# Low parts of the ordinary feed-forward blocks by ScalarE and an adding transfer, and ten more pairs of blocks in seven products

## The chip, the core and the metric

One core of a Trainium2 chip runs the whole kernel. The metric is the device time of one execution in microseconds; three runs of the kernel before gave 1870.56 us at the median (1868.07 to 1871.55). TensorE multiplies, VectorE and ScalarE do elementwise work, GpSimd does a little of it and can issue transfers, SyncE (SP) issues the loads.

## The reference

Two decoder layers over 512 tokens of 1024 channels in float32, batch 1. Each layer is a SwiGLU half-step, a mixer, and another SwiGLU half-step; so there are four feed-forward blocks in all. Every sub-layer is an RMSNorm, a shift and scale from the conditioning vector `c` (adaLN, nine vectors of 1024 a layer, each a 1024 x 1024 product with `c`), and a gated residual add:

```
h = modulate(rms_norm(x, ffn_norm[i, 0]), mod[:, 0, 0], mod[:, 0, 1])
x = x + 0.5 * mod[:, 0, 2][:, None, :] * swiglu(h, w_gate, w_up, w_down)
# swiglu: (silu(h @ w_gate) * (h @ w_up)) @ w_down, d_ff = 2816
```

The mixer of layer 0 is a convolution module beside a gated short convolution, that of layer 1 a causal pooling beside block-sparse attention. A last RMSNorm follows.

## The kernel before

**Numbers.** Activations lie transposed: 8 tiles `x[k]` of 128 channels x 512 tokens. TensorE multiplies in a reduced float32 kind (fp32r), so every operand is split in a high part (a cast) and a low part (the value minus the high part), and a product of two is three matmuls: high x high, high x low, low x high (`mac`, L295).

**Ordinary blocks.** An `Item` is one weight block, K x 128 columns, K = 1024 for gate and up. Two items share one `Raw`, a load of 128 partitions x 2048 floats from HBM into one of four buffers (`RAW_BUFS`), issued on SP's queue in the order in which the plan first touches it; a load goes out only when the buffer of the fourth load before it has been used up. `split` (L270) makes the parts: ScalarE casts the high part (L284), VectorE subtracts for the low part (L286; GpSimd for a few marked ones). The parts have four buffers (`W_BUFS`), and `run` splits up to three items ahead (`AHEAD`) of the one that is multiplied, as soon as the item four back has been emitted. Then come 24 matmuls of 512 columns and `post`: SiLU for gate, the product with it for up (`m`, then its split in `th`, `tl`), the residual for down.

**Pairs.** A gate block and the up block beside it, taken as a 2 x 2 block matrix by the halves of K and by the tokens' halves, can be done in seven products instead of eight (`pair_run`, L817): 84 matmuls of 256 columns instead of 48 of 512. For that VectorE forms sums of weights (`sums13`, `sum2`, `sum4`), splits them, and recombines the results; of the activations `forms` (L717) makes sums once per feed-forward block. The d_ff of 22 blocks of 128 is cut in sections of 8, 6 and 8; in each a number of gate/up blocks, the last ones, go in pairs. The counts before are (0, 2, 8), (2, 6, 8), (2, 4, 8), (2, 6, 8) for the four feed-forward blocks, 56 pairs.

**Order.** Engines run their queues in order, and the order is written out by a plan. `swiglu_pairs` (L948) goes through a feed-forward block: the ordinary gate/up items of a section, then its pair run, then the down items. Beside ordinary items (`beside`) it puts steps of other work for VectorE: the four `forms`, the four `lead_in` steps of the next pair run, and background steps, above all the adaLN products (`ada_steps`, L466: per vector four loads of 1 MB with two VectorE passes each, a fold, a reduce). How many go beside an item is set by a credit in us (3.7 for a gate or up item, 3.5, 2.3 or 2.9 for a down item), from which each step's cost is taken. Around a change of sub-layer `boundary` (L585) weaves the last two down items with the first four items of the next.

Of the kernel before, what the change touches and what calls it, by code (L numbers as in the profile page):

```python
# [42 lines left out]
class Item:  # L43


    def __init__(self, raw, cut, shape, post=None, rhs=None, korder=None, store=None):
        self.raw, self.cut, self.shape = raw, cut, shape
        self.post, self.rhs = post, rhs
        self.korder, self.store = korder, store
        self.hi = self.lo = self.ps = None  # L50
        self.left = 0
        self.pool_low = self.late = self.hold = False
# [16 lines left out]
class Trunk:  # L69
# [183 lines left out]
    def load(self, r):  # L253
        n = 1
        for s in r.shape[1:]:
            n *= s
        t = self.raw.tile([P, 2048], F32, name="raw", tag="raw")[:, 0:n]
        if isinstance(r.src, tuple):
            r.tile = t.rearrange("p (g k c) -> p g k c", g=2, k=ND)
            for g in range(2):  # L260
                self.nc.sync.dma_start(r.tile[:, g], r.src[g])
        elif len(r.shape) == 4:
            r.tile = t.rearrange("p (a b c) -> p a b c", a=r.shape[1], b=r.shape[2])
            for b in range(r.shape[2]):
                self.nc.sync.dma_start(r.tile[:, :, b, :], r.src[:, :, b, :])
        else:
            r.tile = t.rearrange("p (a b) -> p a b", a=r.shape[1])
            self.nc.sync.dma_start(r.tile, r.src)

    def split(self, it):  # L270
# [10 lines left out]
        for i, (hi, lo) in enumerate(parts):  # L281
            w = src[:, i * step:(i + 1) * step, :]
            n = w.shape[1]
            self.nc.scalar.copy(hi[:, 0:n, :], w)  # L284
            eng = self.nc.gpsimd if it.pool_low else self.nc.vector
            low = lambda eng=eng, lo=lo, hi=hi, w=w, n=n: eng.tensor_tensor(  # L286
                lo[:, 0:n, :], w, hi[:, 0:n, :].bitcast(F32), op=ALU.subtract)
            if it.hold:
                self.held.append(low)
            else:  # L290
                low()
            it.hi += [hi[:, a, :] for a in range(n)]
            it.lo += [lo[:, a, :] for a in range(n)]
# [235 lines left out]
    def square(self, k, sl):  # L529

        nc = self.nc
        if k == 0:
            nc.scalar.activation(self.acc[:, sl], self.x[k][:, sl], AF.Square)
            return
        sq = self.np_.tile([P, S], F32, name="sq", tag="sq")
        nc.scalar.activation(sq[:, sl], self.x[k][:, sl], AF.Square)
        if self.ending and k == 7 and sl.start > 0:
            self.sq7 = sq
            return
        self.defer(lambda: nc.vector.tensor_tensor(  # L540
            self.acc[:, sl], self.acc[:, sl], sq[:, sl], op=ALU.add))

    def stats(self, half):
        nc = self.nc
        ps = self.bank()
        for j in range(2):
            c = 2 * half + j
            terms = [self.acc] if half == 0 or not self.ending else [self.acc, self.sq7]
            for t in terms:
                nc.tensor.matmul(ps[:, j:j + 1], lhsT=t[:, c * P:(c + 1) * P], rhs=self.ones[:, 0:1],  # L550
                                 start=t is terms[0], stop=t is terms[-1])
# [95 lines left out]
    def pair(self, src, nk, posts, apart=False, **kw):  # L647

        if apart:
            return [Item(Raw([P, nk, P], src[:, :, j * P:(j + 1) * P], 1), (lambda t: t), (nk, P),  # L650
                         post=posts[j], **kw) for j in range(2)]
        r = Raw([P, nk, 256], src, 2)
        return [Item(r, (lambda t, j=j: t[:, :, j * P:(j + 1) * P]), (nk, P), post=posts[j], **kw)
                for j in range(2)]

    def ffn_items(self, l, s):
# [8 lines left out]
        for n, nf in enumerate(SECTIONS):  # L665
            gu = []
            for fp in range(nf // 2):
# [7 lines left out]
                def up_post(slot):  # L675
                    def go(ps, sl):
# [12 lines left out]
                              apart=apart)  # L689
                u = self.pair(wu[:, :, c0:c0 + 256], ND, [up_post(q) for q in sl_], rhs=self.h_rhs,  # L690
                              apart=apart)
                gu += [g[0], u[0], g[1], u[1]]
            down = []
            for dp in range(ND // 2):
# [3 lines left out]
                    rhs=self.t_rhs)  # L698
# [118 lines left out]
    def pair_run(self, pairs, down):  # L817
# [17 lines left out]
        def keep1(p):  # L835
            p.p1 = self.fp.tile([P, 256], F32, name="p1c", tag="p1c", bufs=1)
# [110 lines left out]

    def swiglu_pairs(self, secs, pairs, bg, skip, fn=None, due=0):  # L948
# [5 lines left out]
        lead = [list(zip(self.lead_in(ps[0]), (2.5, 1.4, 1.9, 1.2))) if ps else [] for ps in pairs]  # L954
        for n, ((gu, down), ps) in enumerate(zip(secs, pairs)):
# [190 lines left out]
    def group_norm(self, r):  # L1146
        nc = self.nc
        _, j, y, stage, x = r
        if stage == 0:
# [4 lines left out]
            r[4] = sq = self.np_.tile([P, S], F32, name="sq", tag="sq")  # L1154
            nc.scalar.activation(sq, y, AF.Square)
        elif stage == 1:
# [9 lines left out]
            r[4] = wide = self.np_.tile([P, S], F32, name="sq", tag="sq")  # L1166
# [115 lines left out]
    def pool_post(self, g):  # L1282
        nc = self.nc

        def go(ps, sl):
# [9 lines left out]
            def mean():  # L1295
                o = self.np_.tile([P, S], F32, name="sq", tag="sq")
# [6 lines left out]
            def mix(o):  # L1303
# [3 lines left out]
                m = self.np_.tile([P, S], F32, name="sq", tag="sq")  # L1307
# [163 lines left out]
    def start_spread(self):  # L1471
# [5 lines left out]
        self.rb0 = self.np_.tile([P, S], F32, name="sq", tag="sq")  # L1477
# [46 lines left out]
    def build(self):  # L1524
# [66 lines left out]
        self.swiglu_pairs(f[0, 0], self.pair_items(0, 0, (0, 2, 8)), bg, 7, AF.Sigmoid, 9)  # L1591
# [46 lines left out]
        bg = steps(1, (2, 0), (2, 2))  # L1638
# [18 lines left out]
        self.swiglu_pairs(f[1, 2], self.pair_items(1, 2, (2, 6, 8)), [], 3)  # L1657
# [102 lines left out]
```

## Time and profile before

| | us |
|---|---|
| median of 3 runs | 1870.56 |
| the profiled execution | 1867.62 |
| its span, first to last instruction | 1865.6 |
| TensorE busy | 1803.4 |
| VectorE busy | 1438.5 |
| ScalarE busy | 802.3 |
| GpSimd busy | 133.9 |

The profile is of one execution. Matmuls are pipelined, so "busy" says that TensorE had work, not that it ran at its peak; what a matmul costs on the path is the distance from its start to the next one's. An engine that waits shows it as idle time, with the instruction that ended the wait behind it. A DMA share of 1 means that all 16 DMA engines moved packets the whole time.

### The profile page before, as it was taken

To read this page: it belongs to the slowest core of one execution; us is meant where nothing else is said; L and a number is where in the kernel's file an instruction comes from. 1 tells how busy PE (TensorE), PEld (TensorE's weight loads), DVE (VectorE), ACT (ScalarE), POOL (GpSimd) and SP (SyncE) were. 2 spreads that over 40 slices of the span, in tenths; PEclk is the share of its full clock that TensorE was granted. 3 is DMA by queue.
4 is the path that set the end of the run, shared out by engine and by line. 5 is a ranking of instruction groups with operands and counts; after the bars stand their busy time and mean duration, and the time that the engine had idled before them with its cause. 6 is when DMAs were issued, how large, how long until landed. Compare 5 with 4: busy or idle time off the path is not lost.

```text
span 1865.6 us, 26636 instructions
## 1 busy us (share of the span) xinstructions
PE 1803.4 (97%) x10730; PEld 1566.0 (84%) x10730; DVE 1438.5 (77%) x2100; ACT 802.3 (43%) x1388; POOL 133.9 (7%) x107
## 2 busy tenths in 40 slices
PE   5999999999979999999999999999999999999998
PEld 4778889988758888989888889998876688898997
DVE  6689779788988868779678787886898577485874
ACT  4322335445544433535344234463545444253543
POOL 2100000005550000000000000000002000000000
PEclk7999999999989999999999999999999999999999
DMA  9585563433232346453423573543362132424321
GB/s 258 169 290 198 161 204 101 136 113 113 68 136 91 113 158 181 133 139 113 149 77 114 191 226 119 156 124 111 125 208 80 45 91 68 113 80 125 91 91 46
DMA packets 263234, 247.52 MB, mean 133 GB/s; under 512 B 5212, under 2 KB 243656, under 8 KB 263112
## 3 DMA queue, kind: packets, MB, share of 16 engines
q1 hardware_dynamic: 262980, 245.78, 42.5%
q8 instruction: 84, 1.38, 0.3%
q14 instruction: 38, 0.31, 0.0%
q10 hardware_dynamic: 132, 0.05, 0.0%
HBM read 243.72 MB, written 2.10 MB: 132 GB/s over the span
## 4 chain that ended last, share of the span: by engine, by line
PE 82%; DVE 12%; ACT 3%; issue 2%; POOL 1%; DMA 0%; SPq 0%; DVEq 0%; ACTq 0%; POOLq 0%
PE bank L784 27%; PE bank L299 17%; PE bank L301 17%; PE bank L300 17%; DVE hl L577 1%; DVE wlo L286 1%; DVE bank L1111 1%; PE bank L1378 1%; DVE wlo L753 1%; DVE t L572 1%; DVE adaacc L484 1%; ACT whi L284 1%; DVE s L762 1%; DVE acc L1501 1%; DVE yb L1043 0%
## 5 line engine op out<-in xcount | busy, mean ns | idle before, releaser
L299 PE MATMUL bank<-th,whi 128*128 128x512 f32 (+1 forms) x896 | 336.3, 375 | 5.2 <-ACT whi L284 4.5
L301 PE MATMUL bank<-th,wlo 128*128 128x512 f32 (+1 forms) x896 | 332.8, 371 | 5.4 <-POOL wlo L286 5.4
L300 PE MATMUL bank<-tl,whi 128*128 128x512 f32 (+1 forms) x896 | 332.8, 371 | 1.1 <-DVE tl L680 0.9
L299 PE MATMUL bank<-hh,whi 128*128 128x512 f32 (+1 forms) x864 | 322.3, 373 | 5.3 <-ACT hh L575 3.2
L300 PE MATMUL bank<-hl,whi 128*128 128x512 f32 (+1 forms) x864 | 316.8, 367 | 8.0 <-DVE hl L577 8.0
L301 PE MATMUL bank<-hh,wlo 128*128 128x512 f32 (+1 forms) x864 | 315.9, 366 | 2.5 <-DVE wlo L286 2.5
L284 ACT CAST whi<-raw 128x1024 fp32r<-128x1024 f32 (+1 forms) x205 | 203.9, 1010 | 136.3 <-PE bank L300 83.2
L286 DVE TENSOR_TENSOR wlo<-raw,whi 128x1024 fp32r<-128x1024 f32 (+1 forms) x195 | 235.0, 1220 | 26.5 <-ACT whi L284 25.7
L301 PEld LDWEIGHTS bank<-th,wlo 128*128 128x128 f32 x896 | 169.0, 189 | 38.5 <-POOL wlo L286 6.6
L299 PEld LDWEIGHTS bank<-th,whi 128*128 128x128 f32 x896 | 169.1, 189 | 38.0 <-ACT whi L284 5.6
L300 PEld LDWEIGHTS bank<-tl,whi 128*128 128x128 f32 x896 | 169.2, 189 | 32.2 <-DVE tl L680 1.3
L300 PEld LDWEIGHTS bank<-hl,whi 128*128 128x128 f32 x864 | 164.0, 190 | 37.9 <-DVE hl L577 9.5
L299 PEld LDWEIGHTS bank<-hh,whi 128*128 128x128 f32 x864 | 163.5, 189 | 37.5 <-ACT hh L575 3.3
L988 DVE SCALAR_TENSOR_TENSOR x<-bank,modG,x 128x512 f32<-128x512 f32 (+1 forms) x124 | 85.7, 698 | 141.1 <-PE bank L301 140.1
L301 PEld LDWEIGHTS bank<-hh,wlo 128*128 128x128 f32 x864 | 163.6, 189 | 32.2 <-DVE wlo L286 3.7
L784 PE MATMUL bank<-f,whi 128*128 128x256 f32 x896 | 163.7, 280 | 11.2 <-ACT yy L843 11.2
L784 PE MATMUL bank<-f,qhi 128*128 128x256 f32 x896 | 165.3, 282 | 0.0
L741 ACT CAST qhi<-raw 128x512 fp32r<-128x512 f32 x168 | 99.4, 618 | 118.4 <-issue 84.4
L784 PEld LDWEIGHTS bank<-f,whi 128*128 128x128 f32 x896 | 136.8, 188 | 13.4 <-ACT yy L843 13.4
L484 DVE SCALAR_TENSOR_TENSOR adaacc<-raw,cond,adaacc 128x1024 f32<-128x1024 f32 x112 | 143.7, 1283 | 2.7
L784 PEld LDWEIGHTS bank<-f,qhi 128*128 128x128 f32 x896 | 138.8, 190 | 0.0
L784 PE MATMUL bank<-f,qlo 128*128 128x256 f32 x448 | 126.4, 282 | 0.0
(245 smaller groups left out, 3317.8 us busy)
## 6 DMA issues: line engine op xcount, KB each, us to landing
raw<-in_ada_w_dram SPq DMA_DIRECT2D x64, 1024.0 KB, 5.3
raw<-in_ffn_w_down_dram SPq DMA_DIRECT2D x32, 1024.0 KB, 5.2
raw<-in_ffn_w_gate_dram SPq DMA_DIRECT2D x58, 512.0 KB, 4.0
raw<-in_ffn_w_up_dram SPq DMA_DIRECT2D x58, 512.0 KB, 5.3
raw<-in_ffn_w_gate_dram SPq DMA_DIRECT2D x15, 1024.0 KB, 5.4
raw<-in_ffn_w_up_dram SPq DMA_DIRECT2D x15, 1024.0 KB, 5.4
raw<-in_ffn_w_down_dram SPq DMA_DIRECT2D x16, 768.0 KB, 4.5
raw<-in_conv_w_in_dram SPq DMA_DIRECT2D x10, 1024.0 KB, 5.0
```

The source lines that it names most:

```text
L284: self.nc.scalar.copy(hi[:, 0:n, :], w)
L286: low = lambda eng=eng, lo=lo, hi=hi, w=w, n=n: eng.tensor_tensor(lo[:, 0:n, :], w, hi[:, 0:n, :].bitcast(F32), op=ALU.subtract)
L299: nc.tensor.matmul(ps, lhsT=it.hi[k], rhs=xh[:, sl], start=start, stop=False)
L300: nc.tensor.matmul(ps, lhsT=it.hi[k], rhs=xl[:, sl], start=False, stop=False)
L301: nc.tensor.matmul(ps, lhsT=it.lo[k], rhs=xh[:, sl], start=False, stop=stop)
L484: nc.vector.scalar_tensor_tensor(acc, r.tile[:, j, :], self.cond[:, k:k + 1], acc, op0=ALU.mult, op1=ALU.add)
L572: nc.vector.scalar_tensor_tensor(t, self.x[k][:, sl], self.modA[:, i, k:k + 1], rb, op0=ALU.mult, op1=ALU.mult)
L577: self.pend = lambda: nc.vector.scalar_tensor_tensor(self.hl[k][:, sl], t, b, self.hh[k][:, sl].bitcast(F32), op0=ALU.add, op1=ALU.subtract)
L741: self.nc.scalar.copy(hi, src)
L753: p.lows[names] = lambda: self.nc.vector.tensor_tensor(lo, src, hi.bitcast(F32), op=ALU.subtract)
L784: mm = lambda w, x, start=False: nc.tensor.matmul(ps, lhsT=w, rhs=x, start=start, stop=False, skip_group_check=True)
L988: nc.vector.scalar_tensor_tensor(self.x[d][:, sl], ps[:, sl], self.modG[:, i, d:d + 1], self.x[d][:, sl], op0=ALU.mult, op1=ALU.add)
```

## The change

`split` gets a third way for marked items (`by_dma`): ScalarE writes the negated cast into the low part's tile, and a transfer issued by GpSimd adds the weights to it, SBUF to SBUF. `swiglu_pairs` marks the gate/up items that are not taken in a boundary and all down items. So that the transfer's source is one row of 4 KB in each partition, ordinary loads are made as two, each of 128 columns (`whole`). The counts of pairs become (0, 4, 8) and three times (4, 6, 8). Where a section has fewer items than steps, `join` puts several steps behind one item. The credits become 4.7 and 4.6, 3.2 or 4.0. One adaLN vector (layer 1, sub-layer 2, scale) moves from the third feed-forward block to the attention. Some scratch tiles change their pool or tag, and the scratch for GpSimd's transfers is 2048 bytes instead of 1024.

```diff
@@ split @@
-            if it.hold:
+            if it.by_dma:
+                self.nc.scalar.activation(lo[:, 0:n, :], w, AF.Copy, scale=-1.0)
+                self.nc.gpsimd.dma_start(lo[:, 0:n, :], w, accum_op=ALU.add)
+            elif it.hold:
                 self.held.append(low)
@@ load @@
-            r.tile = t.rearrange("p (g k c) -> p g k c", g=2, k=ND)
+            r.tile = t.rearrange("p (g k c) -> p g k c", g=2, c=P)
@@ pair @@
-        r = Raw([P, nk, 256], src, 2)
-        return [Item(r, (lambda t, j=j: t[:, :, j * P:(j + 1) * P]), (nk, P), post=posts[j], **kw)
-                for j in range(2)]
+        if whole:
+            r = Raw([P, 2, nk, P], (src[:, :, 0:P], src[:, :, P:2 * P]), 2)
+            cuts = [lambda t, j=j: t[:, j] for j in range(2)]
+        else:
+            r = Raw([P, nk, 256], src, 2)
+            cuts = [lambda t, j=j: t[:, :, j * P:(j + 1) * P] for j in range(2)]
+        return [Item(r, cuts[j], (nk, P), post=posts[j], **kw) for j in range(2)]
@@ ffn_items @@
-                              apart=apart)
+                              apart=apart, whole=(n, fp) > (0, 0))
...
-                    rhs=self.t_rhs)
+                    rhs=self.t_rhs, whole=True)
@@ new @@
+    def join(self, forms, lead, n):
+        gap = n - len(forms) - len(lead)
+        if gap >= 0:
+            return forms + [(None, 0)] * gap + lead
+        out = [(None, 0)] * (n - 4) + lead
+        for e, (fn, cost) in enumerate(forms):
+            k = e * (n - 3) // len(forms)
+            f0, c0 = out[k]
+            if k < n - 4:
+                out[k] = (lambda a=f0, b=fn: (a and a(), b()), c0 + cost)
+            else:
+                last = forms[e:]
+                out[k] = (lambda b=f0: ([f() for f, _ in last], b()), c0 + cost * len(last))
+                break
+        return out
@@ swiglu_pairs @@
+        for it in secs[0][0][max(skip + 1, 4):] + sum((gu * (n > 0) + down for n, (gu, down) in enumerate(secs)), []):
+            it.by_dma = True
...
-                todo = forms + [(None, 0)] * (len(gu) - 8) + todo
-            self.beside(gu, todo, bg, 3.7)
+                todo = self.join(forms, todo, len(gu))
+            self.beside(gu, todo, bg, 4.7)
...
-                        2.9 if last else 3.5 if nf == 8 else 2.3)
+                        4.0 if last else 4.6 if nf == 8 else 3.2)
@@ square, keep1, group_norm, pool_post, start_spread: tiles @@
-        sq = self.np_.tile([P, S], F32, name="sq", tag="sq")
-        nc.scalar.activation(sq[:, sl], self.x[k][:, sl], AF.Square)
+        if sl == FULL:
+            sq = self.fp.tile([P, S], F32, name="yy", tag="yy", bufs=2)
+        else:
+            sq = self.np_.tile([P, 256], F32, name="sq", tag="sq")
+        nc.scalar.activation(sq, self.x[k][:, sl], AF.Square)
...
-            p.p1 = self.fp.tile([P, 256], F32, name="p1c", tag="p1c", bufs=1)
+            p.p1 = self.np_.tile([P, 256], F32, name="t256", tag="t", bufs=3)
@@ build @@
-        self.swiglu_pairs(f[0, 0], self.pair_items(0, 0, (0, 2, 8)), bg, 7, AF.Sigmoid, 9)
+        self.swiglu_pairs(f[0, 0], self.pair_items(0, 0, (0, 4, 8)), bg, 7, AF.Sigmoid, 9)
...
-        self.swiglu_pairs(g0, self.pair_items(0, 2, (2, 6, 8)), bg, 3)
+        self.swiglu_pairs(g0, self.pair_items(0, 2, (4, 6, 8)), bg, 3)
...
-        bg = steps(1, (1, 1), (1, 0), (1, 2), (2, 1))
-        self.swiglu_pairs(f[1, 0], self.pair_items(1, 0, (2, 4, 8)), bg, 3, AF.Exp)
+        bg = steps(1, (1, 1), (1, 0), (1, 2))
+        self.swiglu_pairs(f[1, 0], self.pair_items(1, 0, (4, 6, 8)), bg, 3, AF.Exp)
...
-        bg = steps(1, (2, 0), (2, 2))
+        bg = steps(1, (2, 1), (2, 0), (2, 2))
...
-        self.swiglu_pairs(f[1, 2], self.pair_items(1, 2, (2, 6, 8)), [], 3)
+        self.swiglu_pairs(f[1, 2], self.pair_items(1, 2, (4, 6, 8)), [], 3)
...
-                    dynamic_dma_scratch_size=1024)
+                    dynamic_dma_scratch_size=2048)
```

## Rows read from the trace of the kernel before

**Rows 1.** Page: busy us, share of span, instructions; then the chain by engine
```profile
PE 1803.4 (97%) x10730; PEld 1566.0 (84%) x10730; DVE 1438.5 (77%) x2100; ACT 802.3 (43%) x1388; POOL 133.9 (7%) x107
...
PE 82%; DVE 12%; ACT 3%; issue 2%; POOL 1%; DMA 0%; SPq 0%; DVEq 0%; ACTq 0%; POOLq 0%
```
**Rows 2.** Waits of TensorE: engine, line, awaited; us in total, times, longest
```profile
PE bank L784 <- ACT yy L843: 11.2, 11, 2.8
PE bank L300 <- DVE hl L577: 8.0, 6, 1.6
```
**Rows 3.** Windows: stretch, length, busy us by engine, PEclk, DMA share, GB/s
```profile
620.00:630.00 10.00, 10.00 (x44) 8.07 (x43) 9.65 (x18) 3.74 (x7) 0.00 (x0) 1.00 0.31 107
295.00:305.00 10.00, 10.00 (x88) 10.00 (x87) 9.09 (x13) 5.97 (x13) 0.00 (x0) 1.00 0.40 107
```
**Rows 4.** Windows of the first feed-forward block
```profile
95.00:105.00 10.00, 10.00 (x44) 8.04 (x43) 8.83 (x9) 2.83 (x4) 0.00 (x0) 1.00 1.05 376
140.00:150.00 10.00, 9.80 (x43) 7.99 (x44) 9.45 (x15) 2.11 (x2) 0.00 (x0) 1.00 1.00 349
83.40:147.00 63.60, 62.65 (x271) 50.21 (x272) 56.40 (x71) 18.99 (x25) 0.00 (x0) 1.00 0.81 282
```
**Rows 5.** Timeline of ScalarE in a pair run: start us, us, instruction
```profile
300.48 0.37 ACT L837 COPY p1c<-bank 128x256 f32<-128x256 f32 x1
...
310.30 0.37 ACT L837 COPY p1c<-bank 128x256 f32<-128x256 f32 x1
```
**Rows 6.** Timeline of TensorE in ordinary items
```profile
621.43 0.40 PE L299 MATMUL bank<-hh,whi 128*128 128x512 f32 x1
...
626.33 0.39 PE L299 MATMUL bank<-hh,whi 128*128 128x512 f32 x1
```
**Rows 7.** Page, costliest groups: xcount, busy us, mean ns, idle before
```profile
L284 ACT CAST whi<-raw 128x1024 fp32r<-128x1024 f32 (+1 forms) x205 | 203.9, 1010 | 136.3 <-PE bank L300 83.2
L286 DVE TENSOR_TENSOR wlo<-raw,whi 128x1024 fp32r<-128x1024 f32 (+1 forms) x195 | 235.0, 1220 | 26.5 <-ACT whi L284 25.7
...
L484 DVE SCALAR_TENSOR_TENSOR adaacc<-raw,cond,adaacc 128x1024 f32<-128x1024 f32 x112 | 143.7, 1283 | 2.7
```
**Rows 8.** Page, DMA issues: xcount, KB each, median us to landing
```profile
raw<-in_ffn_w_gate_dram SPq DMA_DIRECT2D x58, 512.0 KB, 4.0
```
**Rows 9.** Timeline of ScalarE at the start of the second feed-forward block
```profile
610.25 2.00 ACT L284 CAST whi<-raw 128x1024 fp32r<-128x1024 f32 x2
```
**Rows 10.** Timeline of TensorE there
```profile
615.13 0.39 PE L299 MATMUL bank<-hh,whi 128*128 128x512 f32 x1
615.36 0.40 PE L300 MATMUL bank<-hl,whi 128*128 128x512 f32 x1
615.60 0.39 PE L301 MATMUL bank<-hh,wlo 128*128 128x512 f32 x1
```
**Rows 11.** Timeline of SP's queue, first feed-forward block
```profile
69.18 14.63 SPq L268 DMA_DIRECT2D raw<-in_ada_w_dram  x2
...
141.31 0.37 SPq L268 DMA_DIRECT2D raw<-in_ffn_w_down_dram  x1
```
**Rows 12.** Timeline of TensorE, first matmul of the seventh down block
```profile
169.22 0.39 PE L299 MATMUL bank<-th,whi 128*128 128x512 f32 x1
```
**Rows 13.** Windows in the attention
```profile
1400.00:1420.00 20.00, 20.00 (x82) 13.56 (x81) 17.66 (x37) 10.25 (x24) 10.35 (x9) 1.00 0.19 65
1420.00:1440.00 20.00, 20.00 (x83) 13.79 (x82) 14.48 (x31) 11.62 (x26) 1.43 (x1) 1.00 0.18 54
```

More of the change, by code (lines that the diff above doesn't have):

```diff
@@ L51, in __init__ @@
         self.left = 0
-        self.pool_low = self.late = self.hold = False
+        self.pool_low = self.late = self.hold = self.by_dma = False
 class Pair:
@@ L540, in square @@
         self.defer(lambda: nc.vector.tensor_tensor(
-            self.acc[:, sl], self.acc[:, sl], sq[:, sl], op=ALU.add))
+            self.acc[:, sl], self.acc[:, sl], sq, op=ALU.add))
     def stats(self, half):
@@ L549, in stats @@
             for t in terms:
-                nc.tensor.matmul(ps[:, j:j + 1], lhsT=t[:, c * P:(c + 1) * P], rhs=self.ones[:, 0:1],
+                e = j if t is not self.acc else c
+                nc.tensor.matmul(ps[:, j:j + 1], lhsT=t[:, e * P:(e + 1) * P], rhs=self.ones[:, 0:1],
                                  start=t is terms[0], stop=t is terms[-1])
@@ L645, in t_rhs, with pair @@
         return self.th[k], self.tl[k]
-    def pair(self, src, nk, posts, apart=False, **kw):
+    def pair(self, src, nk, posts, apart=False, whole=False, **kw):
         if apart:
@@ L688, in ffn_items @@
                 g = self.pair(wg[:, :, c0:c0 + 256], ND, [gate_post(q) for q in sl_], rhs=self.h_rhs,
-                              apart=apart)
+                              apart=apart, whole=(n, fp) > (0, 0))
                 u = self.pair(wu[:, :, c0:c0 + 256], ND, [up_post(q) for q in sl_], rhs=self.h_rhs,
-                              apart=apart)
+                              apart=apart, whole=(n, fp) > (0, 0))
                 gu += [g[0], u[0], g[1], u[1]]
@@ L1153, in group_norm @@
             self.free(ps)
-            r[4] = sq = self.np_.tile([P, S], F32, name="sq", tag="sq")
+            r[4] = sq = self.fp.tile([P, S], F32, name="sqw", tag="sqw", bufs=2)
             nc.scalar.activation(sq, y, AF.Square)
@@ L1165, in group_norm @@
             nc.gpsimd.tensor_tensor(rs, ms, self.mhalf, op=ALU.pow)
-            r[4] = wide = self.np_.tile([P, S], F32, name="sq", tag="sq")
+            r[4] = wide = self.fp.tile([P, S], F32, name="sqw", tag="sqw", bufs=2)
             nc.scalar.copy(wide.rearrange("p (a b) -> p a b", a=8), rs[:, :, None].to_broadcast([P, 8, 64]))
@@ L1295, in mean @@
             def mean():
-                o = self.np_.tile([P, S], F32, name="sq", tag="sq")
+                o = self.fp.tile([P, S], F32, name="sqw", tag="sqw", bufs=2)
                 nc.vector.scalar_tensor_tensor(o, cur[:, 16:], 1.0 / w, u[:, 16:],
@@ L1306, in mix @@
                 b, sc = self.at["pool_b"] + g, self.at["pool_scale"] + g
-                m = self.np_.tile([P, S], F32, name="sq", tag="sq")
+                m = self.fp.tile([P, S], F32, name="sqw", tag="sqw", bufs=2)
                 nc.vector.tensor_scalar(m, po, self.vec[:, b:b + 1], self.vec[:, sc:sc + 1],
@@ L1476, in start_spread @@
                                 self.rs[0][:, c:c + 1].to_broadcast([P, P]), self.ident)
-        self.rb0 = self.np_.tile([P, S], F32, name="sq", tag="sq")
+        self.rb0 = self.fp.tile([P, S], F32, name="yy", tag="yy", bufs=2)
         nc.scalar.copy(self.rb0, ps)
```

## The prediction

> **What bounds the kernel now.** I read the page's busy times and its chain of waits first. TensorE is busy 97% of the span and holds 82% of the chain [rows 1]; the reader is to see that nothing else is near. The list of what TensorE waited for then shows how little idle time there is: the longest entry is 11.2 us in 11 waits of the `f` products, the next 8.0 us [rows 2]. So a gain has to come from fewer TensorE columns. VectorE is the engine that limits how many blocks can go in seven products: in a run of pairs it is busy 9.09 of 10 us, and in the ordinary stretch of the first section 9.65 of 10 [rows 3]. The share of the DMA engines is the third view: small on average, but in the first feed-forward block it is 1.05 at 376 GB/s in one stretch of 10 us and 1.00 at 349 GB/s in another [rows 4]. The change takes load off VectorE and puts it on the DMA engines, so the question is what that costs there.
>
> **The seven products: the gain.** In the run of eight pairs the copy of p1 comes once a pair: from 300.48 to 310.30 us is 9.82 us a pair [rows 5]. An ordinary gate or up block is 24 matmuls of 512 columns. From 621.43 to 626.33 us are 21 of them, 0.233 us each, so two blocks take 48 x 0.233 = 11.20 us [rows 6]. The saving is 1.38 us a pair. The counts go from 10+16+14+16 = 56 to 12+18+18+18 = 66 pairs: 10 x 1.38 = 13.8 us less on TensorE, all of it on the path. The number of pair runs stays 11, so the stall of the first pair of each run (the 11 waits above) stays too.
>
> **The low parts: off VectorE, on ScalarE.** With `by_dma` an item's low part is a second ScalarE pass (1.01 us by the high part's row) in place of 1.22 us of VectorE [rows 7], and a transfer issued by GpSimd. Marked and run are 8+4+24 items in the first block (gate/up of two sections, and all down blocks) and 4+24 in each of the other three, 120 in all: 146 us leave VectorE, 121 us come to ScalarE, which is busy 43% [rows 1]. I cost ScalarE's part at nothing where splits run three items ahead (16.8 us), and VectorE's relief also at nothing: TensorE did not wait for it there, and the credit per item (3.7 to 4.7 us and so on) fills the relief with the adaLN steps that lost their places. Adding up those credits by the code, every step still finds a place before its end. GpSimd waits for ScalarE at each issue; behind that stand only the two small powers of the statistics and the third head block's low part, which come after the last marked items of a block.
>
> **The adding transfer itself.** Its kind does not stand in the trace. The nearest rows are loads: 512 KB lands 4.0 us after issue at the median [rows 8]; at the full-share rates of [rows 4] (349 to 376 GB/s) 512 KB holds the 16 engines for 1.45 us. An add needs source and destination, so up to two such passes: 2.9 us. Ends therefore 1.45 and 2.9 us of the engines, landing after 4.0 to 5.4 us. At nothing I do not put the low end: the bytes have to move; what could make it nothing on the path is idle DMA time.
>
> **Where the transfer is waited for.** At a block's start the first marked item's buffer becomes free only when TensorE is done with the first head item. In the trace of before, ScalarE's cast of it begins at 610.25 (two casts in a row of 2.00 us), and TensorE wants its low part at 615.60 [rows 9, 10]. In the changed order cast and negated copy end at 612.3, which leaves 3.3 us for a landing of 4.0 to 5.4: 0.7 to 2.1 us late, in three blocks 2 to 6.3 us. I take 6. It covers another squeeze: five items now have to carry eight steps that had nine items (four `forms` at 4.6 us and four lead-in steps, 25.4 us by the code's own costs, behind the first item's end), 22.4 us of TensorE; what VectorE is late there, 2 to 3 us, falls into the same wait. Later items have 11 us or more, the first down block of a run nearly 10: no wait at landings up to 7 us.
>
> **The first feed-forward block.** Here the sum of DMA time decides. From 83.4 us to 147.0 the DMA share was 0.81, so 51.5 us of the engines, for 11 adaLN loads and 6 weight loads of 1 MB, the last of which, for the last two down blocks, was issued at 141.31 [rows 4, 11]: 3.0 us a load. The changed code asks for more before that same weight load: by the credits 16 adaLN loads precede it, one of them already issued at 69.18, so 4 more, 12 us. Weight rows shrink from 1 KB to 512 bytes (two loads of 512 KB): 10 us at a share of 0.40 and 107 GB/s where rows have 512 bytes, against 0.31 for the same bytes in 1 KB rows [rows 3], 0.9 us a MB, 5 us for six. And 13 adding transfers, 19 to 38 us. Together 87.5 to 106.5 us. The seventh down block's products begin at 169.22 [rows 12]; back from there 2 us of ScalarE and 5.4 of landing, so its load must be in by about 162: 78.6 us. The engines are over-asked by 9 to 28 us, and because loads share four buffers in program order, weights cannot pass the adaLN loads. I take 14, nearer the low end: a load's 3.0 us holds waits for HBM, which a transfer inside SBUF may fill. Elsewhere the demand fits: the other blocks have 5.6 us an item and at most one adaLN load for each.
>
> The Trainium skill, "Collectives: The Full Stack", section "The bandwidth ceiling: the fold count and why AG ≠ RS ≠ AR", says that an add in the DMA engines is slower than a copy because it takes two source reads, pushed through one read queue. No run here shows it yet. By it the estimate is the upper end, 28 us in this stretch, and the sum below would be 23 us over; by the copy rows alone it would be the lower one, 9 us.
>
> **The moved adaLN set.** One more set (eight VectorE passes of up to 1.28 us [rows 7], by the code's costs a fold of 2.8 and a reduce of 0.9: 13.9 us) runs beside the attention, reaching to about 1420 us. VectorE is there busy 17.66 of 20 us, then 14.48 [rows 13]. It falls behind by up to 11 us and needs to be in time only two units (some 8 us) later. 0 to 11 us late; I take 3. Tags and scratch size move no work: nothing. The second issue of each weight load is 0.37 us more on SP's queue [rows 11], which stands idle between loads: nothing.
>
> **Sum.** -13.8 + 6 + 14 + 3 = +9.2 us on the profiled execution's 1867.6 us. That execution stands 2.9 us under the median 1870.56, so against the median 1880.
>
> **Rivals.**
> (a) The transfers hide, and the change is faster. Place: the same stretch of the first block. Of its first 63.6 us 19% of DMA time is free [rows 4], and the share goes over 1.00, so transfers inside SBUF may run while loads wait for HBM; if an adding transfer costs the loads under about 0.7 us, the over-demand falls to 2 us or less, and with landings of 4.0 us: -13.8 + 2 + 2 + 1 = -8.8, 1862. For it: the relief of VectorE is real and TensorE's saving certain. Against: the full stretches of [rows 4].
> (b) One pass per transfer, nothing hidden: -13.8 + 2 + 9 + 1 = -1.8, 1869: no change.
> (c) Two full passes: -13.8 + 6.3 + 28 + 3 = +23.5, 1894. Should a transfer land after more than 7 us, each pair run's end waits as well.
> (d) The change does not carry its pairs: adaLN steps left over at a block's end would be done with TensorE idle, 2.6 us each. The credits speak against it; I give it no share of its own.
>
> **How the numbers follow.** Forecast 0.36, (a) 0.33, (b) 0.14, (c) 0.17. Under 0.2% (3.7 us, about what a measurement of this kernel tells from no change) lies (b) with its edges: 0.14. Faster 0.33, slower 0.53. The forecast's own range is 1875 to 1888. For eight in ten I reach from 1860, near (a)'s value with its best edge (every unknown at its low end and no over-demand: -11.8) left out, to 1898, past (c) but short of all upper ends together (-13.8 + 6.3 + 28 + 11 = +31.5).
>
> **What would show it.** Right: most of the loss before 180 us; from 95 to 165 us the DMA share near 1.0 throughout, TensorE waiting for low parts that a DMA brought or for weights, VectorE waiting for adaLN loads; pair periods unchanged at 9.8 us; at each later block's start one wait of 1 to 2 us of the L301 products. Wrong: adding packets of under half the time of a 4 KB load, no idle TensorE before 180 us, and the saving of 13.8 us bare; or waits at every down block, which would make it worse than (c).

## The result and the profile after

The changed kernel takes 1936.96 us (median of 4 runs, 1936.07 to 1938.48) where the kernel before took 1871.05 beside it (4 runs, 1868.07 to 1871.96): a ratio of 1.0356 (95% interval 1.0338 to 1.0374). It is 66 us slower. The prediction had the sign, but 1880 us for the time and 1898 as its upper end. The profiled execution has a span of 1934.3 us, 68.7 over that of before.

From the page of the kernel after: busy time by engine; the granted clock and the DMA share in 40 slices; two DMA queues with packets, MB and share of 16 engines; the chain by engine.

```profile
PE 1819.0 (94%) x11090; PEld 1591.4 (82%) x11090; DVE 1362.5 (70%) x2060; ACT 932.4 (48%) x1578; POOL 239.2 (12%) x227
...
PEclk7998998999989999999999999999999999999999
DMA  9799866482224548495665775848265125836463
...
q1 hardware_dynamic: 331684, 245.79, 43.2%
q0 software_dynamic: 17280, 58.73, 16.2%
...
PE 59%; DVE 14%; DMA 11%; issue 7%; ACT 4%; POOL 1%; SPq 0%; DVEq 0%; POOLq 0%; ACTq 0%
```

TensorE's share of the chain fell from 82% to 59%, and transfers, which held 0% of it [rows 1], hold 11%. VectorE is 76 us less busy and ScalarE 130 more: the work moved as planned. The new queue q0, that of the adding transfers, holds the 16 engines for 16.2% of 1934.3 us, 313 us in 120 transfers, 2.6 us each; counted in pieces of 512 KB (88, and 32 of 384 KB) it is 313 / 112 = 2.8 us.

What TensorE waited for in the kernel after (engine, line, awaited; us in total, times, longest):

```profile
PE bank L304 <- DMA wlo<-raw: 22.9, 12, 7.2
PE bank L795 <- DVE wlo L764: 10.7, 4, 4.1
...
PE bank L303 <- DVE tl L691: 7.7, 1, 7.7
PE bank L795 <- ACT yy L854: 6.1, 9, 1.0
...
PE bank L506 <- DVE adar L501: 5.9, 2, 5.5
```

The longest entry of before, the `yy` wait [rows 2], has become shorter. Beside it now stand low parts that a transfer brings late (the first row), and results of VectorE that are late (rows two, three and five). The same view over all engines says why VectorE is late:

```profile
DVE adaacc L487 <- DMA raw<-in_ada_w_dram: 55.9, 20, 8.2
```

Its adaLN passes waited 55.9 us for their own loads, in 20 waits; before, these passes had 2.7 us of idle time ahead of them in all [rows 7].

The windows of the first block, after, with a fourth over its full stretch, and one each out of the down blocks of the second and the third feed-forward block (columns as in [rows 3]: PEclk, DMA share and GB/s are the last three):

```profile
95.00:105.00 10.00, 10.00 (x44) 8.08 (x43) 3.17 (x3) 2.30 (x3) 0.00 (x0) 1.00 1.06 302
140.00:150.00 10.00, 10.00 (x41) 7.87 (x39) 7.16 (x12) 1.04 (x2) 0.86 (x1) 0.92 1.07 265
83.40:147.00 63.60, 55.19 (x226) 43.87 (x225) 38.02 (x47) 22.80 (x29) 8.64 (x10) 0.92 1.06 302
82.00:210.00 128.00, 108.20 (x440) 85.47 (x441) 86.15 (x126) 47.55 (x58) 16.57 (x19) 0.92 1.05 297
740.00:760.00 20.00, 20.00 (x87) 16.10 (x87) 10.61 (x10) 3.06 (x3) 1.63 (x2) 1.00 1.05 296
1220.00:1240.00 20.00, 17.70 (x82) 13.98 (x80) 11.50 (x17) 4.00 (x6) 0.93 (x2) 1.00 1.11 312
```

Against [rows 4] the share over 83.4 to 147 us rose from 0.81 to 1.06, and it stays full to 210 us. A busy VectorE of 8.83 of 10 us has become 3.17: it stands and waits for loads. The two later stretches are as full. Where a block's low parts are the transfers' and adaLN loads run too, the DMA engines have nothing left.

The chain of waits of the kernel after in that block (start us, us, what held the end):

```profile
131.86 8.67 DMA raw<-in_ada_w_dram
...
140.63 1.30 DVE adaacc L487
141.95 1.28 DVE adaacc L487
143.26 11.46 DMA raw<-in_ada_w_dram
154.75 1.29 DVE adaacc L487
156.06 1.30 DVE adaacc L487
...
160.16 0.61 DVE tl L691
...
171.50 9.37 DMA wlo<-raw
```

The reader is to see how background work comes onto the path: an adaLN load takes 8.67 and then 11.46 us to land, VectorE stands at the pass that wants it, and queued behind that pass is `tl`, the low part of an activation that TensorE's next products need (TensorE waits 7.7 us for it). The adding transfer at 171.50 takes 9.37 us to land.

Waits are not all of it. The granted clock of the kernel before and of the kernel after:

```profile
core 0: 1865.6 us, clock 0.989
```
```profile
core 0: 1934.3 us, clock 0.972
```

Added up from the gaps between its instructions in the trace, TensorE stood idle 54.3 us before and 107.7 after, 53.4 more (from its first instruction to its last). And its busy time is 15.6 us longer (1819.0 against 1803.4 in [rows 1]), though 13.8 us of columns are gone by the count: 29.4 us of slower products. Some 25 of them are the clock's, as an estimate: TensorE was busy at the lower of its two levels (1.2 of 2.4 GHz) for 73.9 us, before for 23.8, and half of the 50 more is lost. The other 4 stay open. 53.4 + 29.4 - 13.8 = 69.0, near the 68.7 of the spans.

By blocks (a boundary is the first `rs<-ms` of its statistics on GpSimd), the first feed-forward block is 33.7 us longer than before, the convolution 3.4, the second block 14.3, the third 9.0, the attention 9.5, the last block 1.3 shorter. The table below uses the same boundaries.

### The profile page after: what moved, and what is told of

It is laid out like the page before. It is cut to its first block, busy times and chain, and to the rows that moved or that the text cites. A ratio compares the mean times of both kernels' runs of the same rounds, so it can differ in the third digit from the quotient of the medians.

```text
span 1934.3 us, 28024 instructions
## 1 busy us (share of the span) xinstructions
PE 1819.0 (94%) x11090; PEld 1591.4 (82%) x11090; DVE 1362.5 (70%) x2060; ACT 932.4 (48%) x1578; POOL 239.2 (12%) x227
## 3 DMA queue, kind: packets, MB, share of 16 engines
q1 hardware_dynamic: 331684, 245.79, 43.2%
q0 software_dynamic: 17280, 58.73, 16.2%
## 4 chain that ended last, share of the span: by engine, by line
PE 59%; DVE 14%; DMA 11%; issue 7%; ACT 4%; POOL 1%; SPq 0%; DVEq 0%; POOLq 0%; ACTq 0%
PE bank L795 30%; PE bank L304 9%; PE bank L302 9%; PE bank L303 9%; DMA wlo<-raw 4%; DMA raw<-in_ffn_w_up_dram 3%; DMA raw<-in_ada_w_dram 2%; DVE adaacc L487 2%; DMA raw<-in_ffn_w_down_dram 2%; DVE wlo L286 1%; DVE bank L1141 1%; DVE hl L584 1%; DVE wlo L764 1%; ACT whi L284 1%; DVE x L1018 1%
## 5 line engine op out<-in xcount | busy, mean ns | idle before, releaser
L302 PE MATMUL bank<-hh,whi 128*128 128x512 f32 (+1 forms) x704 | 262.6, 373 | 5.4 <-ACT hh L582 3.2
L304 PE MATMUL bank<-hh,wlo 128*128 128x512 f32 (+1 forms) x704 | 256.0, 364 | 11.6 <-DMA wlo<-raw 9.0
L303 PE MATMUL bank<-hl,whi 128*128 128x512 f32 (+1 forms) x704 | 256.4, 364 | 8.4 <-DVE hl L584 8.4
L290 POOL DMA_DIRECT2D wlo<-raw x120 | 104.8, 873 | 1262.0 <-ACT t L848 764.7
L795 PE MATMUL bank<-f,whi 128*128 128x256 f32 x1056 | 195.8, 283 | 6.1 <-ACT yy L854 6.1
L795 PE MATMUL bank<-f,qhi 128*128 128x256 f32 x1056 | 195.3, 283 | 0.5 <-ACT qhi L752 0.5
L487 DVE SCALAR_TENSOR_TENSOR adaacc<-raw,cond,adaacc 128x1024 f32<-128x1024 f32 x112 | 145.2, 1297 | 58.6 <-DMA raw<-in_ada_w_dram 55.9
L304 PEld LDWEIGHTS bank<-hh,wlo 128*128 128x128 f32 x704 | 135.8, 193 | 36.8 <-DMA wlo<-raw 11.6
L303 PEld LDWEIGHTS bank<-hl,whi 128*128 128x128 f32 x704 | 135.9, 193 | 31.8 <-DVE hl L584 9.9
L302 PEld LDWEIGHTS bank<-hh,whi 128*128 128x128 f32 x704 | 136.2, 193 | 30.4 <-ACT hh L582 3.3
L795 PE MATMUL bank<-f,wlo 128*128 128x256 f32 x528 | 150.8, 286 | 10.7 <-DVE wlo L764 10.7
```

Source lines behind the costliest of these rows:

```text
L290: self.nc.gpsimd.dma_start(lo[:, 0:n, :], w, accum_op=ALU.add)
L302: nc.tensor.matmul(ps, lhsT=it.hi[k], rhs=xh[:, sl], start=start, stop=False)
L303: nc.tensor.matmul(ps, lhsT=it.hi[k], rhs=xl[:, sl], start=False, stop=False)
L304: nc.tensor.matmul(ps, lhsT=it.lo[k], rhs=xh[:, sl], start=False, stop=stop)
L487: nc.vector.scalar_tensor_tensor(acc, r.tile[:, j, :], self.cond[:, k:k + 1], acc, op0=ALU.mult, op1=ALU.add)
L795: mm = lambda w, x, start=False: nc.tensor.matmul(ps, lhsT=w, rhs=x, start=start, stop=False, skip_group_check=True)
```

## The experiments

Each kernel is the changed one with an edit, where nothing else is said; where a text says "as before" or "the kernel before", the edit is shown against the kernel before. Changes of the blocks' lengths against the profiled execution of before, in us, from one profiled execution each (executions of the same work differ by some 4 us in the convolution and the second block, for a reason shown in the last section, and by up to 1.5 in the others):

```
                        block 1  conv  block 2  block 3  attention  block 4
after                    +33.7   +3.4   +14.3    +9.0     +9.5      -1.3
small adaLN loads         +8.9   +4.8    -2.2    -3.3     +9.4      -1.4
small adding transfers   +12.0   +1.7    -6.6    -5.1     +9.2      -0.7
transfer reads high part +29.2   +1.7    +7.3    +5.4     +9.0      -1.4
66 pairs, no relief       +3.2   +3.6    -3.2    -2.0     +8.9      -1.6
moved set alone           +0.2   +4.7    -0.1    -0.5     +9.4      -0.3
rows of 512 bytes alone   +0.1   +0.3    +4.3    -0.3     -0.4      -0.3
last block by VectorE     -1.4   +0.3    +4.1     0.0     +0.1      -1.3
transfers in last block   -1.5    0.0    +0.3    -0.3     -0.4      -1.3
lows by GpSimd           +11.2   +3.6    +0.3    +1.7     +9.0      +1.9
four more pairs           +0.1   +4.4    -3.7    -0.3     -0.4      -1.6
six more pairs            +0.1   +4.4    -3.6    +1.1     +0.1      -1.3
```

**The adaLN loads shrunk.** They bring one eighth of their bytes; VectorE's passes keep their sizes and read that eighth repeatedly.

```diff
+                    src = r.tile[:, j, None, :].to_broadcast([P, 8, P])
...
-            r = Raw([P, 2, D], w[:, 2 * kk:2 * kk + 2, c0:c0 + D], 1)
+            r = Raw([P, 2, P], w[:, 2 * kk:2 * kk + 2, c0:c0 + P], 1)
```

> The changed kernel, with adaLN loads of an eighth of their bytes (128 of 1024 columns, read eight times over by VectorE in passes as long as before, so the shift and scale values are left out). Theory: the DMA engines are over-asked where adaLN loads and adding transfers run together. Then the loss in the first three feed-forward blocks goes: the DMA share there falls under 0.8, the waits for adaLN loads (55.9 us of VectorE) and for wlo are nearly gone, and the time is 1871 - 14 for the pairs + some 9 for the attention, so 1862 to 1875 us. Rival, buffers held by the transfers until they land: little changes, 1915 to 1935. Rival, VectorE overfilled by the raised credits: 1930 to 1940.

Measured: 1882.87 us, ratio 1.0085 (1.0056 to 1.0114). 54 of the 66 us are gone (52 by the blocks' lengths), with every adding transfer in its place. It is 8 us over the upper end of the theory; the table has 8.9 in the first block.

**The adding transfers shrunk** to 128 of 1024 columns; GpSimd issues as many, ScalarE's two passes stay.

```diff
-                self.nc.gpsimd.dma_start(lo[:, 0:n, :], w, accum_op=ALU.add)
+                self.nc.gpsimd.dma_start(lo[:, 0:1, :], w[:, 0:1, :], accum_op=ALU.add)
```

> The changed kernel, with adding transfers over 128 of an item's 1024 columns (the other low parts stay the negated high parts, so those are left out). Issue, order and waits stay; the engines' time for a transfer falls from 2.6 us to about 0.4, the landing from 6.7 us to 3 or 4. Theory, engine time: 1871 - 14 + 9 and a few us for loads in 512-byte rows, 1866 to 1880 us. Rival, the buffers held: half of the loss stays, since issue and receipt stay, 1890 to 1915. Rival, VectorE overfilled: 1930 to 1940.

Measured: 1874.38 us, ratio 1.0044 (1.0018 to 1.007). 63 us are gone (58 by the blocks' lengths). The two sum to 117 us, far more than the loss: neither stream costs it by itself, it is both at once. The second and third block are shorter than before in either kernel; in the first 8.9 and 12.0 us stay. The windows of the second block's stretch say it, first for the small adaLN loads, then for the small adding transfers:

```profile
740.00:760.00 20.00, 18.74 (x154) 18.27 (x153) 18.90 (x29) 9.21 (x18) 0.00 (x0) 1.00 0.61 158
```
```profile
740.00:760.00 20.00, 18.73 (x160) 18.54 (x159) 18.82 (x27) 10.80 (x21) 0.00 (x0) 1.00 0.59 153
```

The share is 0.61 and 0.59 where it was 1.05. A stretch at one time holds earlier or later work in a faster kernel; the blocks' lengths above are free of that.

**The transfer reads the high part** instead of the loaded weights, same bytes: the load's buffer comes free after ScalarE's two passes, without waiting for the transfer's landing.

```diff
-                self.nc.gpsimd.dma_start(lo[:, 0:n, :], w, accum_op=ALU.add)
+                self.nc.gpsimd.dma_start(lo[:, 0:n, :], hi[:, 0:n, :].bitcast(F32), accum_op=ALU.add)
```

> The changed kernel, but the transfer adds the high part in place of the weights (the low part comes out with the wrong sign). Same bytes and rows, but the load's buffer is free as soon as ScalarE is done, some 7 us earlier. Theory, engine time: no change, 1930 to 1940 us. Rival, the buffers held until the transfer lands keep SP's next loads back: most of the loss goes, 1875 to 1900.

Measured: 1918.99 us, ratio 1.0278 (1.0248 to 1.0308). That is between the theory and its rival: 18 us of the 66 hang on the four load buffers being held until a transfer has landed, 48 remain without that.

**66 pairs without any of the relief**: counts, raised credits and the moved set as in the change, all low parts by VectorE, 1 KB rows.

```diff
-                    rhs=self.t_rhs, whole=True)
+                    rhs=self.t_rhs, whole=False)
...
-            it.by_dma = True
+            it.by_dma = False
```

> The changed kernel with its 66 pairs and its credits, but every low part by VectorE as before, and ordinary loads in one piece with 1 KB rows: no adding transfer, 120 x 1.22 us more on VectorE. Theory, engine time of the DMA: the DMA share stays under 1 in the first block; what is lost is VectorE's overfill, up to 1.22 us for each of some 45 items with full credits, so 1890 to 1920 us, with TensorE waiting for VectorE and not for DMA. Rival, that the raised credits are what costs in the changed kernel: here it must be far worse than 1937.

Measured: 1877.35 us, ratio 1.0048 (1.0025 to 1.007). The 1890 to 1920 us expected of a VectorE with too much to do did not come. Blocks two to four are shorter than before by 3.2, 2.0 and 1.6 us, without an engine taking anything from VectorE. The first is 3.2 longer: TensorE waits there once for `tl` of VectorE. First this wait, then VectorE's timeline up to it:

```profile
PE bank L303 <- DVE tl L691: 4.8, 1, 4.8
```
```profile
137.24 0.69 DVE L689 TENSOR_TENSOR m<-bank,sg 128x512 f32<-128x512 f32 x1
137.85 2.60 DVE L487 SCALAR_TENSOR_TENSOR adaacc<-raw,cond,adaacc 128x1024 f32<-128x1024 f32 x2
...
143.17 0.68 DVE L691 TENSOR_TENSOR tl<-m,th 128x512 fp32r<-128x512 f32 x1
```

No load is late here. Two adaLN passes and a fold, 5.3 us, stand in the queue between `m` and the `tl` that is made from it; before, no fold stood there and the wait was 0.9 us. That the raised credits put them there is argued from the code; no run has the raised credits alone.

**The moved adaLN set alone**: pairs, credits and VectorE's low parts as before, only the set in the attention (and the new tile tags).

```diff
-        bg = steps(1, (1, 1), (1, 0), (1, 2), (2, 1))
+        bg = steps(1, (1, 1), (1, 0), (1, 2))
...
-        bg = steps(1, (2, 0), (2, 2))
+        bg = steps(1, (2, 1), (2, 0), (2, 2))
```

> The kernel before (its pairs, credits, loads and low parts by VectorE), with two things of the change alone: the adaLN set of layer 1 (sub-layer 2, scale) moved to the attention, and the scratch tiles' new pools and tags. Theory: the attention is as late as in the changed kernel, 9 us (203.7 us between its boundaries against 194.2), since VectorE there has no room for a set more; 1875 to 1881 us. Rival, that the adding transfers or the clock after waits made the attention late: 1866 to 1872.

Measured: 1876.43 us, ratio 1.0048 (1.003 to 1.0065); the attention is 9.4 us longer, as in every kernel that has the move. From 1380 to 1450 us, first the kernel before, then this one with TensorE's waits in that stretch:

```profile
1380.00:1450.00 70.00, 69.92 (x290) 47.62 (x289) 58.04 (x117) 35.08 (x85) 13.43 (x10) 1.00 0.34 110
```
```profile
1380.00:1450.00 70.00, 64.84 (x257) 44.41 (x256) 64.58 (x121) 29.61 (x72) 13.95 (x10) 0.95 0.45 149
```
```profile
PE bank L1335 <- DVE tl L1414: 2.7, 1, 2.7
PE bank L1335 <- DVE sqw L1330: 2.4, 1, 2.4
```

VectorE, at 58 of 70 us, takes 6.5 more; TensorE has 5.1 us of waits, and the granted clock falls to 0.95 over the stretch, 3.5 us missing, part of it perhaps in the waits. The new tile tags are not the cause: the next kernel has them, and its attention is no longer than before.

**Rows of 512 bytes alone**: pairs and VectorE's low parts as before, gate, up and down loads in two issues of 512-byte rows.

```diff
-        r = Raw([P, nk, 256], src, 2)
+        r = Raw([P, 2, nk, P], (src[:, :, 0:P], src[:, :, P:2 * P]), 2)
```

> The kernel before with ordinary loads made as two of 512-byte rows, and the scratch tiles' new pools and tags; low parts by VectorE, no adding transfer, no moved set. Theory: loads take some 43 us more of the DMA engines over the whole run, which find room: 1867 to 1874 us, nothing above 5 us in any block. If the new tags cost something in the convolution (188.2 us in the changed kernel against 184.8), it shows here too. Rival, that the short rows are what over-asks the engines: 1885 or more.

Measured: 1870.99 us, ratio 1.0008 (0.9997 to 1.0019). Nothing, though q1 now holds 44.8% of 1869.6 us where it held 42.5% of 1865.6: 45 us more of the 16 engines for the same bytes, which find room. What these rows cost beside transfers, where there is no room, was not run by itself; the kernel with small adding transfers has them too.

**Two more pairs in the last block alone**, the rest as before, low parts by VectorE, then **the same with adding transfers** and their 512-byte rows there. The last block has no adaLN steps.

```diff
-        self.swiglu_pairs(f[1, 2], self.pair_items(1, 2, (2, 6, 8)), [], 3)
+        self.swiglu_pairs(f[1, 2], self.pair_items(1, 2, (4, 6, 8)), [], 3)
```

> The kernel before with two more pairs in the last feed-forward block alone ((4, 6, 8), with the joined steps), low parts by VectorE; the scratch tiles as changed. No adaLN step runs there. Two pairs save 2.8 us, the joined steps cost 1 to 2: 1.6 us less than the kernel before as in the run with 66 pairs and no transfer, 1864 to 1870 us. Rival, that ten more blocks need VectorE's relief: 2 us or more slower than before.

> The change in the last feed-forward block alone (18 pairs, low parts of 28 items by ScalarE and adding transfers, 512-byte rows), where no adaLN loads run; the other blocks and the sets' places as before. Theory (transfers cost time only where adaLN loads run beside them): that block saves 2.8 us for two pairs, gives back 1 to 2 us at its start, and the kernel takes 1867 to 1871 us where the kernel before takes 1870. Rival (each transfer costs some 0.6 us of the path wherever it stands: 66 + 13.8 us over 120 transfers): 28 x 0.6 - 2.8 = 14 us more, 1884.

Measured: 1868.53 us by VectorE (0.9994, 0.9983 to 1.0005) and 1870.00 with 28 transfers (0.9994, 0.9984 to 1.0004); in both the block is 1.3 us shorter. TensorE waits for a transfer once, at the block's start, as this row of the second kernel's waits from 1500 us on shows; then its queue of adding transfers:

```profile
PE bank L304 <- DMA wlo<-raw: 1.6, 1, 1.6
```
```profile
q0 software_dynamic: 4032, 13.63, 4.0%
```

Each transfer holds the engines as long as in the changed kernel (4.0% of 1861.6 us for 26 pieces of 512 KB, 2.9 us a piece). So 28 transfers without adaLN loads cost nothing measurable beyond what VectorE's low parts cost; a price of some 0.6 us on each is out.

**The low parts by GpSimd**: the plan of the change, but the marked items are subtracted by GpSimd; no transfer, no negated copy, 1 KB rows.

```diff
-                self.nc.scalar.activation(lo[:, 0:n, :], w, AF.Copy, scale=-1.0)
-                self.nc.gpsimd.dma_start(lo[:, 0:n, :], w, accum_op=ALU.add)
+                self.nc.gpsimd.tensor_tensor(lo[:, 0:n, :], w, hi[:, 0:n, :].bitcast(F32), op=ALU.subtract)
```

> The changed kernel, but the low parts of the 120 marked items are subtracted by GpSimd (2.37 us each for 128x1024 in the trace of before): VectorE's relief, the 66 pairs, the credits and the moved set stay; the adding transfers, ScalarE's negated copies and the 512-byte rows go. Theory (the transfers' time on the DMA engines beside the adaLN loads is the loss): -13.8 for the pairs, +9.4 for the moved set, 0 to 6 in the first block for its raised credits: 1865 to 1872. Rival (the low parts' way round VectorE is itself the loss, since the item's buffer is held 1.2 us longer and TensorE waits at each block's start): 2.37 us in place of VectorE's 1.22, with waits of 1 to 2 us at three block starts and raw buffers freed later: 1875 to 1885. Second rival (GpSimd's passes slow VectorE's beside them): VectorE's mean 1.22 us rises and the kernel goes over 1880.

Measured: 1896.36 us, ratio 1.0143 (1.0124 to 1.0162). My theory missed by 24 us; the second rival's mechanism shows. VectorE's adaLN passes with GpSimd's subtracting beside them, and then the same passes in the kernel of 66 pairs without relief (page, groups: xcount, busy us, mean ns):

```profile
L486 DVE SCALAR_TENSOR_TENSOR adaacc<-raw,cond,adaacc 128x1024 f32<-128x1024 f32 x112 | 174.7, 1560 | 4.5 <-DMA raw<-in_ada_w_dram 1.6
L484 DVE TENSOR_SCALAR adaacc<-raw,cond 128x1024 f32<-128x1024 f32 x16 | 16.2, 1010 | 0.0
```
```profile
L487 DVE SCALAR_TENSOR_TENSOR adaacc<-raw,cond,adaacc 128x1024 f32<-128x1024 f32 x112 | 145.1, 1296 | 2.9
L485 DVE TENSOR_SCALAR adaacc<-raw,cond 128x1024 f32<-128x1024 f32 x16 | 11.9, 745 | 0.0
```

1296 ns have become 1560 in the mean, and 745 ns 1010: 34 us more of VectorE. This run is no clean test of the relief, since it took part of it back. How the 19 us over the kernel without relief divide between that and later low parts stays open.

**Four more pairs, nothing else**: the kernel before with 18 pairs in the second and the last block, the second block's credits raised by 1.0 us an item. Then **six more**, with two in the third block (0.6 us an item).

```diff
-        self.swiglu_pairs(g0, self.pair_items(0, 2, (2, 6, 8)), bg, 3)
+        self.swiglu_pairs(g0, self.pair_items(0, 2, (4, 6, 8)), bg, 3, more=1.0)
...
-        self.swiglu_pairs(f[1, 2], self.pair_items(1, 2, (2, 6, 8)), [], 3)
+        self.swiglu_pairs(f[1, 2], self.pair_items(1, 2, (4, 6, 8)), [], 3)
```

> A version drawn from the runs so far: the kernel before, its tiles, its adaLN steps in their places, low parts by VectorE, no transfer; two more pairs in the second and in the last feed-forward block, with joined steps, credits raised by 1 us in the second. In the run without transfers these two blocks were 3.3 and 1.6 us shorter than before. So 4 to 5 us under the kernel before, 1862 to 1866 us if that stands at 1867 to 1870. Rival, VectorE's overfill takes the gain back: within 2 us of the kernel before.

> The kernel of four more pairs (low parts by VectorE, 1 KB rows, no adding transfer, no moved set) with two more in the third feed-forward block, whose adaLN credit is raised by 0.6 us an item: 62 pairs. Theory (VectorE had room for them, a pair saves 1.38 us): 2.8 us under the 1862.4 of four more pairs, 1859 to 1861. Rival (VectorE without relief is full in that block with four adaLN sets, so its fold and split passes make TensorE wait): no gain over four more pairs, 1862 to 1868.

Measured: 1862.35 us with four more (0.9962, 0.9948 to 0.9976), which beats both kernels, by 0.4% and by 3.9%; 1865.81 with six more (0.9977, 0.9966 to 0.9988). Not all of the second block's 3.7 us is columns: the waits for `yy` at its pair runs are 3.9 us in place of 6.5. The last two pairs gave nothing, as the rival had it: the third block is 1.1 us longer than before, with one wait of 3.4 us for `yy` where the longest was 0.9, and the lower clock for 3.4 us behind it. That VectorE, with four adaLN sets there, is what this wait hangs on was not shown.

## Why the prediction was wrong, point by point

**The seven products: right.** The copy of p1 in a pair run after, against [rows 5]:

```profile
364.10 0.36 ACT L848 COPY t<-bank 128x256 f32<-128x256 f32 x1
373.92 0.36 ACT L848 COPY t<-bank 128x256 f32<-128x256 f32 x1
```

9.82 us again. With no relief the second to fourth block are 3.2, 2.0 and 1.6 us shorter, of 2.8, 5.5 and 2.8 by the count. The stalls of the first pairs stay in sum, 11.9 us in 11 waits there against 11.2, but not in place: 3.9, 3.9 and 2.1 us in these blocks where they were 6.5, 2.1 and 1.4.

**The block-start wait: right.** The transfer issued at 651.98 us lands after 4.62 us, and the low part's first matmul waits 1.75 us for it (the chain, then TensorE's timeline, at the second block's start):

```profile
651.98 4.62 DMA wlo<-raw
```
```profile
656.64 0.50 PE L304 MATMUL bank<-hh,wlo 128*128 128x512 f32 x1 [1.75 <-DMA wlo<-raw]
```

The others are 1.4 and 1.5 us; 0.7 to 2.1 was forecast. A wait of 1.6 us for VectorE's `hl`, which stands ahead of each block before [rows 2], stays.

**The transfer's price: the wrong end taken.** One pass was put at 1.45 us of the engines, two at 2.9; measured are 2.8, and 2.9 in the last block alone. The page cited in the prediction, the Trainium skill, "Collectives: The Full Stack", section "The bandwidth ceiling: the fold count and why AG ≠ RS ≠ AR", says of the reduce step of a collective that its add takes two source reads; the trace agrees for this add, 313 us for 112 pieces of 512 KB. I took 14 us over-demand in the first block, because loads might leave gaps that a transfer fills. They leave none: the share is 1.05 over 128 us. The upper end was 28.

**The first block: right in place, and in the main in mechanism, too small in size.** It lost 33.7 + 2.8 = 36.5 us. TensorE's waits of over 1 us from 82 us to the block's end are 2.9, 5.5, 2.3, 7.7, 1.1 and 7.2, together 26.7, where before had none. What I left out is what comes with a wait: the granted clock was 0.92 over the 128 us from 82 to 210, 10 us missing, and 0.68 over 296 to 312, 5 more. Part of that lies in the waits themselves. The lower level was granted for 31 us of the block, 17 of them with TensorE busy; half of those, 9 us, is lost, as an estimate. 26.7 + 9 make nearly all of the 36.5.

Not all of it is the DMA engines'. With the loads shrunk 8.9 us remain in this block, with the transfers shrunk 12.0, with neither transfers nor relief 3.2, and in all three the longest wait is the one for `tl`; 4.8 us without transfers, and with the loads and then the transfers shrunk:

```profile
PE bank L303 <- DVE tl L692: 5.8, 1, 5.8
```
```profile
PE bank L303 <- DVE tl L691: 9.4, 1, 9.4
```

So the adaLN steps ahead of `tl`, which the prediction put at nothing, delay it even where no load is late, and a late load adds to that. How the 7.7 us in the changed kernel divide was not separated. Of the signs, "most of the loss before 180 us" did not come: by VectorE's fifth addition of a down block to `x`, at 190.8 us where it was at 164.4, 26 of the 66 us are lost.

**"Elsewhere the demand fits: the other blocks have 5.6 us an item and at most one adaLN load for each": this step failed.** No sum stood behind it. By the prediction's own prices a down item asks 1.5 us for its 512 KB of weights (half of 3.0 a MB), 3.0 for one adaLN load and 1.45 to 2.9 for its transfer: 6.0 to 7.4 us in 5.6, over-asked at both ends. Measured: share 1.05 and 1.11 in these stretches, and 14.3 + 2.8 = 17 us lost in the second block, 9.0 + 5.5 = 14.5 in the third, 31.6 us where only the waits at the two blocks' starts, 4 us, were put. The last block, with transfers and no adaLN load, lost 1.5, its start alone. "No wait at landings up to 7 us" fell with it: landings were 6.7 and 7.8 us at the median,

```profile
wlo<-raw POOLq DMA_DIRECT2D x88, 512.0 KB, 6.7
...
wlo<-raw POOLq DMA_DIRECT2D x32, 384.0 KB, 7.8
```

and 9.4 in full stretches, and the load buffer held until then delays the loads behind (18 us, by the third experiment). TensorE's two longest waits for a transfer, 7.2 us at 296.4 and 5.1 at 849.4, stand amid the down blocks of a second section. An item there is 18 matmuls, 4.2 us, and by the same prices asks 5.2 to 6.3 for its 384 KB. The transfer of the second wait, in the chain:

```profile
845.69 10.64 DMA wlo<-raw
```

**VectorE's relief at nothing: right, and more than that.** It was not needed for the eight pairs of the second, third and last block: with raised credits and no relief, and one adaLN set moved away from the third, these gain. In the first block the steps that the credits place were not free, as said above.

**The moved set: within 0 to 11, the value too low.** 9.4 measured, 3 taken. 5.1 us are waits for VectorE, and the lower clock added most of the rest.

**The rivals.** Two full passes (c) had the right mechanism at 1894 and stopped at the first block. (a), that transfers hide, holds only without adaLN loads beside them. Of the 57 us between forecast and result the first block has 36.5 - 14, the second and third 31.6 less the 4 put for their starts, the attention 9.5 - 3: together 56.6; the 3.4 us of the convolution and the small differences of the last block are left out.

## What to carry to other kernels

When work is moved from an engine to the DMA engines, make the sum of their time for each stage, an item at a time, with every stream that runs there, background loads too, and an adding transfer at two passes; the average (43.2% and 16.2% here) says nothing about it. Late background loads come onto the path through an in-order engine: what is queued behind the pass that waits is what TensorE misses. And test first whether the relief is needed: the kernel with four more pairs and none of it is the fastest here.

## What the runs showed of the hardware that was not expected

An adding transfer inside SBUF holds the 16 engines for 2.8 us per 512 KB with 4 KB rows, and GpSimd for 0.87 us to issue it.

With GpSimd's 128x1024 subtracting beside them, VectorE's adaLN passes take 264 ns more in the mean (1296 to 1560), and the subtracting itself takes 2.53 us for these items, 2.37 for the ten others of that kernel.

In or after many waits of TensorE the granted clock falls to the lower level, 1.2 of 2.4 GHz, for some us. In the kernel after, windows that begin with two of its waits (7.7 and 3.5 us long; PEclk is the third column from the end):

```profile
153.00:166.00 13.00, 5.26 (x14) 4.12 (x14) 9.63 (x11) 1.43 (x2) 1.09 (x2) 0.61 1.08 308
...
1139.00:1149.00 10.00, 6.47 (x32) 6.22 (x32) 9.82 (x17) 3.06 (x6) 0.00 (x0) 0.66 0.82 210
```

But the same wait doesn't always do it. In the second block the kernel before and the kernel of 512-byte rows have the same two waits of 2.8 us for `yy`. The stretch with the first of them, before and then with 512-byte rows:

```profile
727.00:747.00 20.00, 17.19 (x147) 16.99 (x146) 19.01 (x24) 9.22 (x18) 0.00 (x0) 1.00 0.41 109
```
```profile
729.00:749.00 20.00, 17.19 (x124) 17.00 (x123) 16.27 (x21) 8.87 (x17) 0.00 (x0) 0.83 0.40 106
```

TensorE is busy 17.19 of 20 us in both, but with 147 matmuls at a clock of 1.00 and 124 at 0.83. With a second fall, to 0.91 behind the other wait, that is the 4.3 us by which this block is longer there, at equal work of TensorE. The kernel before by itself spreads as far: 25 executions took 1865.4 to 1873.5 us, at granted clocks of 0.990 to 0.986. So differences of 4 us between single executions in this block, and in the convolution, need be no effect of an edit; and a wait that is taken away can be worth nearly twice its length (5.6 us of waits here, and 4.3 of lower clock with them). What decides whether the clock falls was not found.
